# Linear attention rounds of a decoder layer: memory values as 512-column products in banks of their own, a norm by whole banks, three memory parts behind the last round, and early splits of the attention output

## The chip, the cores and the metric

The kernel runs on one core of one Trainium2 chip. Its time is the device time of one execution in microseconds (us). Before the change it is 1370.31 us, the median of 3 runs (1368.11 to 1372.6).

The core has engines that run side by side, each with its own instruction queue: PE (TensorE, matmuls; its weight loads are listed apart as PEld), DVE (VectorE), ACT (ScalarE), POOL (GpSimd) and SP (SyncE, which here only issues DMAs). PE writes to PSUM, eight banks of 128 partitions x 512 fp32 columns; DVE and ACT read them. DMA moves data between device memory and SBUF.

## The reference

```python
def reference(x, mem, norm_mix, w_in, ...):
    hn = rms_norm(h, norm_mix[l])
    gq, gk, gv, gr, ga, sq, sk, sv = jnp.split(hn @ w_in[l], split_at, axis=-1)
    o_gla = gla_mixer(gq, gk, gv, gr, ga, w_alpha[l], b_alpha[l], gla_gain[l])
    o_swa = swa_mixer(sq, sk, sv, rel_bias, sinks[l])
    h = h + jnp.concatenate([o_gla, o_swa], axis=-1) @ w_out[l]
    h = h + cross_attn(rms_norm(h, norm_cross[l]), rms_norm(mem, norm_mem[l]),
                       w_q_c[l], w_k_c[l], w_v_c[l], w_o_c[l])
    h = h + conv_ffn(rms_norm(h, norm_ffn[l]), w_up[l], conv_w[l], conv_b[l], w_down[l])
    return rms_norm(h, norm_final)

def gla_mixer(q, k, v, r, a_low, ...):       # chunks of 64 tokens, 4 heads, d_k 64, d_v 128
    ...                                      # o_intra = masked (q k) v,  o_inter = q S,  S = decay * S + k v
    o = o * lax.rsqrt(jnp.mean(o * o, axis=-1, keepdims=True) + EPS) * gla_gain
    return o.reshape(B, T, GLA_VW) * jax.nn.silu(r)
```

The layer has 1024 tokens and a width of 1024; `mem` has 256 tokens. All is fp32. Cross-attention needs `memn @ w_k` and `memn @ w_v`, 256 x 1024 each, which depend on `mem` and the weights only.

## The kernel before, in words

**Products.** Each fp32 operand is split into a high and a low part (`split`, L109 to L113: an ACT cast or scaled copy makes the high part, a DVE subtract the low part), and each product is three matmuls (`mm3`, L136 to L138: high x high, high x low, low x high). Weights come through three stage buffers `st` (`load`, L121) and are split from there into slots `w` that hold three loads. PSUM banks are handed out by role: F, S and O in the part of the program that is spoken of here (2, 4 and 2 banks).

**Stages.** First come x, its transposes and the products of its rows (`rows_a`); then the sliding-window attention in blocks of 128 queries (`swa`), whose PE order is written out by hand and in which the column products of the linear attention (`cols_gla`) fill the gaps. `swa_values` makes a block's output in one O bank, copies it to SBUF (L813) and stores it to `ow_d` with two POOL DMAs. `gate_silu` puts SiLU on the gates. Then come the gates and decays of the linear attention (`gla_gates`, `gla_decays`, L540 to L591) beside the products of the remaining value columns (`rows_b`), then `gla`.

**Rounds.** `gla` works on two blocks of 128 tokens at a time: four rounds. A round's output products (`gla_products`, L677 and L684) fill two F banks `po`. Then PE makes the states and the masked attention of the next round (L639, L662; DVE turns them into `S` at L646 and `att` at L666). `gla_norm` takes the sums of squares of the eight 128 x 128 pieces on ACT (L184), an inverse root (L170 to L178) and eight scaled copies `o` on ACT (L699). `gla_output` transposes `o` on PE (L712), multiplies by gain and gate on DVE (L715) and splits the result into `x` tiles.

**Memory parts.** `memory` is a generator. Up to its first `yield` it loads the 256 rows of `mem`, transposes and splits them (L314 and the splits L112, L113 with the gain `norm_mem`), and broadcasts the inverse roots of the rows to `mbc` (L332 on PE, a copy on ACT). After that, each `next(memory)` issues one part: eight parts for the values (four column blocks of 256, and in each the two halves of the memory tokens) and eight for the keys (four heads, two halves each). A part is 24 matmuls of 256 columns into one half of an O bank, both halves of a bank one after the other, then a split of this half and a POOL DMA to `v_d` or `k_d`. The value splits are scaled by the rows' inverse roots; a key half is first multiplied by `mbc` on DVE. In the rounds three parts stand ahead of the transposes of the round before, and one behind them; no part stands behind the last round's norm.

**Order.** On PE the order of `swa` and of the rounds is the written one (`manual_schedule`). Elsewhere, and on the other engines, a scheduler sets the order ahead of time; the chip then runs each queue in that order, and an instruction that waits holds up all that are behind it on its engine.

**After the rounds.** `swa_mix` loads the output of the sliding-window attention back in four loads of 512 KB and splits it (L109, L110); `mix_out` multiplies by `w_out` (L136 to L138 `psF<-x,w`, eight column blocks in two halves), each block's weights loaded through `st`. Cross-attention, the feed-forward network and the final norm follow.

Of the kernel before, what the change touches and what calls it, by code (L numbers as in the profile page):

```python
# [17 lines left out]
F32 = mybir.dt.float32  # L18
# [8 lines left out]
P = 128  # L27
# [33 lines left out]
class Layer:  # L61
# [237 lines left out]
    def memory(self, new):  # L299


        nc, a = self.nc, self.a
        rows = []
        for i in range(2):
            t = self.stage((P, T))
            nc.sync.dma_start(out=t, in_=a["mem"][0, i * P:(i + 1) * P, :])
            rows.append(t)
        parts = [[new("wg", [P, 3, MEM], F32R, 8) for _ in range(3)] for _ in range(2)]
# [9 lines left out]
        ssq = self.small("mssq", [P, 2], bufs=1)  # L318
        r = self.small("mrs", [P, 2], bufs=1)
        for i in range(2):  # L320
            self.sumsq(rows[i], ssq[:, i:i + 1], T)
        self.rsqrt(r, ssq, D, 2)
# [3 lines left out]
        def save(d, part, t):  # L326
# [3 lines left out]
        ps = self.bank("O")  # L330
        for i in range(2):
            nc.tensor.matmul(ps[:, i * P:(i + 1) * P], rhs=self.ident, start=True, stop=True,  # L332
                             lhsT=r[:, i:i + 1].to_broadcast([P, P]))
        bc = new("mbc", [P, MEM])
        nc.scalar.copy(out=bc, in_=ps[:, :MEM])
        yield
        wv = a["w_v_c"][0].rearrange("(kt p) c -> p kt c", p=P)
        for c in range(4):
            w = [self.load([(lambda t: t, wv[:, 4 * g:4 * g + 4, 256 * c:256 * c + 256])], (P, 4, 256), parts=2)
                 for g in range(2)]  # L340
            ps = self.bank("O")
            for i in range(2):
                tk = slice(i * P, (i + 1) * P)
                out = ps[:, i * MEM:(i + 1) * MEM]
                for k in range(NK):
                    wh, wl = w[k // 4]
                    self.mm3(out, mh[k][:, tk], ml[k][:, tk], wh[:, k % 4], wl[:, k % 4], k == 0, k == NK - 1)
                t = new("la", [P, 2, MEM], F32R, 4)
                self.split(out, t[:, 0], t[:, 1], r[:, i:i + 1])
                save(self.v_d[c], i, t)  # L350
                yield
        for h in range(4):
            ps = self.bank("O")
            for d in range(2):
                wh, wl = self.load_cols(a["w_k_c"][0], (2 * h + d) * P)
                out = ps[:, d * MEM:(d + 1) * MEM]
                for k in range(NK):
                    self.mm3(out, wh[:, k], wl[:, k], mh[k], ml[k], k == 0, k == NK - 1)
# [1068 lines left out]
```

## Time and profile before

| what | value |
|---|---|
| median of 3 runs | 1370.31 us (1368.11 to 1372.6) |
| the profiled execution | 1371.46 us, its span 1369.7 us |
| PE busy | 1324.6 us, 97% of the span |
| DVE, ACT, POOL busy | 903.2, 601.6, 73.6 us (66%, 44%, 5%) |
| gates, decays and `rows_b` | 243 to 295 us of the span |
| transposes of `mem` and first states | 295 to 301.4 us |
| the four rounds with the memory parts | 301.4 to 374.3 us |
| last norm, ahead of the last transposes | 374.3 to 384.6 us |
| `mix_out` begins | 387.59 us |

A view by windows gives, for a stretch of the span, the busy time of each engine with the number of its instructions, then the granted PE clock (1.00 is full speed), the share of the DMA engines' time and the rate in GB/s. A row of the timeline gives the start, the busy time, the engine, the line, the operation, out<-in and the shapes; in square brackets stands the idle time of the engine just before, and what released it. A row of the waits gives the total idle time, how often, and the longest. A row of groups gives, behind the count, the busy time and the mean in ns of one.

### The profile page before, as it was taken

Reading aid. Unit: us, or ns where it says so; the run is one execution under the profiler, and the core shown is the slowest. Engines: PE = TensorE matmul, PEld = TensorE weight load, DVE = VectorE, ACT = ScalarE, POOL = GpSimd, SP = SyncE. Lnnn points to the kernel's source line nnn. Section 1 sums busy time; section 2 is a strip of 40 time slices with the busy share of each in tenths; the row PEclk is TensorE's granted clock in tenths of the full one; section 3 lists DMA queues with packets and bytes.
Section 4 is the critical chain, followed back from the end, with each engine's and each line's share of the span. In section 5 each row is a group of like instructions: output and inputs, shape, how many; then the busy total and the mean of one; then the engine's idle time right before and its main releaser. Section 6 shows DMA issues by size and latency. Waiting matters only on the chain.

```text
span 1369.7 us, 17685 instructions
## 1 busy us (share of the span) xinstructions
PE 1324.6 (97%) x6735; PEld 1101.6 (80%) x6735; DVE 903.2 (66%) x1590; ACT 601.6 (44%) x1134; POOL 73.6 (5%) x126
## 2 busy tenths in 40 slices
PE   5999999999879999999999999999999999999997
PEld 5887777898868888887888888888888887888785
DVE  4626653636744543345448998888888887997776
ACT  5604443616633333345333544444444444454455
POOL 3100000001100100000110000000000000000000
PEclk9999999999989999999999999999999999999999
DMA  8441110315474421124321243322212228810204
GB/s 268 113 118 55 44 39 16 97 55 177 151 174 145 162 92 62 46 75 134 86 82 40 75 159 104 102 85 92 91 65 82 87 92 291 307 62 3 75 16 147
DMA packets 142094, 142.71 MB, mean 104 GB/s; under 512 B 15394, under 2 KB 111800, under 8 KB 142008
## 3 DMA queue, kind: packets, MB, share of 16 engines
q1 hardware_dynamic: 131446, 108.92, 26.1%
q0 software_dynamic: 9376, 30.54, 6.3%
q10 hardware_dynamic: 1186, 2.12, 0.4%
q8 instruction: 53, 0.87, 0.3%
q14 instruction: 33, 0.27, 0.1%
HBM read 106.93 MB, written 36.18 MB: 104 GB/s over the span
## 4 chain that ended last, share of the span: by engine, by line
PE 90%; DVE 4%; ACT 2%; DMA 2%; issue 1%; SPq 1%; POOL 0%; ACTq 0%; DVEq 0%; POOLq 0%
PE psS L1063 14%; PE psF L1063 13%; PE psF L136 12%; PE psF L138 12%; PE psF L137 12%; PE psF L1170 4%; PE psS L1170 4%; PE psO L136 2%; PE psT L1170 2%; PE psO L1170 2%; PE psO L137 2%; PE psO L138 1%; PE psS L136 1%; PE psS L138 1%; PE psS L137 1%; DVE w L110 1%
## 5 line engine op out<-in xcount | busy, mean ns | idle before, releaser
L109 ACT CAST w<-st 128x1024 fp32r<-128x1024 f32 (+2 forms) x171 | 144.5, 847 | 294.2 <-PE psF L137 137.4
L110 DVE TENSOR_TENSOR w<-st,w 128x1024 fp32r<-128x1024 f32 (+2 forms) x171 | 165.6, 971 | 97.4 <-ACT w L109 96.4
L136 PE MATMUL psF<-x,w 128*128 128x512 f32 x336 | 133.7, 398 | 0.4 <-DVE eb L715 0.4
L138 PE MATMUL psF<-x,w 128*128 128x512 f32 x336 | 132.2, 393 | 0.0
L137 PE MATMUL psF<-x,w 128*128 128x512 f32 x336 | 132.0, 393 | 0.0
L1092 DVE SCALAR_TENSOR_TENSOR uy<-uy,vec,uy 128x1023 f32<-128x1023 f32 (+1 forms) x88 | 112.1, 1280 | 1.0 <-ACT uy L1090 0.4
L1170 PE MATMUL psF<-w,w 128*128 128x512 f32 x330 | 92.8, 391 | 0.6 <-DVE w L110 0.6
L1170 PE MATMUL psS<-w,w 128*128 128x512 f32 x330 | 92.3, 390 | 0.0
L1063 PE MATMUL psS<-a,w 128*128 128x512 f32 x360 | 86.5, 389 | 0.0
L1063 PEld LDWEIGHTS psS<-a,w 128*128 128x128 f32 x360 | 67.6, 188 | 14.0
L1063 PE MATMUL psF<-a,w 128*128 128x512 f32 x324 | 77.8, 389 | 0.0
L136 PEld LDWEIGHTS psF<-x,w 128*128 128x128 f32 x336 | 63.7, 190 | 16.6 <-issue 3.1
L138 PEld LDWEIGHTS psF<-x,w 128*128 128x128 f32 x336 | 63.5, 189 | 14.4 <-issue 0.6
L137 PEld LDWEIGHTS psF<-x,w 128*128 128x128 f32 x336 | 63.8, 190 | 12.7
L1170 PEld LDWEIGHTS psF<-w,w 128*128 128x128 f32 x330 | 61.8, 188 | 14.3 <-DVE w L110 1.3
L1170 PEld LDWEIGHTS psS<-w,w 128*128 128x128 f32 x330 | 62.0, 188 | 12.8
L1063 PEld LDWEIGHTS psF<-a,w 128*128 128x128 f32 x324 | 60.8, 188 | 12.6
L136 PE MATMUL psF<-act,w 128*128 128x512 f32 x176 | 69.7, 396 | 0.0
L137 PE MATMUL psF<-act,w 128*128 128x512 f32 x176 | 69.1, 393 | 0.0
L138 PE MATMUL psF<-act,w 128*128 128x512 f32 x176 | 68.8, 391 | 0.0
L1090 ACT ACTIVATE uy<-uy,vec 128x1024 f32<-128x1024 f32 x44 | 54.8, 1246 | 24.7 <-DVE uy L1083 16.9
L1063 PE MATMUL psS<-act,w 128*128 128x512 f32 x240 | 57.8, 389 | 0.0
(367 smaller groups left out, 2867.1 us busy)
## 6 DMA issues: line engine op xcount, KB each, us to landing
st<-in_w_up_dram SPq DMA_DIRECT2D x44, 512.0 KB, 5.0
g_d<-uy POOLq DMA_DIRECT2D x22, 512.0 KB, 2.9
act<-in_w_down_dram SPq DMA_DIRECT2D x12, 512.0 KB, 8.5
st<-g_d SPq DMA_DIRECT2D x10, 512.0 KB, 4.5
res<-g_d SPq DMA_DIRECT2D x10, 512.0 KB, 9.5
st<-in_w_in_dram SPq DMA_DIRECT2D x9, 512.0 KB, 4.6
xt_d<-pts POOLq DMA_DIRECT2D x16, 256.0 KB, 3.1
st<-in_w_v_c_dram SPq DMA_DIRECT2D x8, 512.0 KB, 3.4
```

The source lines that it names most:

```text
L109: h = nc.scalar.copy(out=hi, in_=src)
L110: l = nc.vector.tensor_tensor(out=lo, in0=src, in1=hi.bitcast(F32), op=ALU.subtract)
L136: mm(out, lhsT=lh, rhs=rh, start=start, stop=False)
L137: mm(out, lhsT=lh, rhs=rl, start=False, stop=False)
L138: mm(out, lhsT=ll, rhs=rh, start=False, stop=stop)
L1063: nc.tensor.matmul(ps, lhsT=b[l][:, q], rhs=a[q][r], start=first and q == 0 and n == 0, stop=first and q == 3 and n == 2, skip_group_check ...
L1090: nc.scalar.activation(out=y, in_=u, func=AF.Identity, scale=self.v("cw2", j), bias=self.v("conv_b", j))
L1092: nc.vector.scalar_tensor_tensor(out=y[:, s:], in0=u[:, :T - s], scalar=self.v(nm, j), in1=y[:, s:], op0=ALU.mult, op1=ALU.add)
L1170: nc.tensor.matmul(ps[i], lhsT=g[:, l, tk], rhs=w[:, r], start=first and k == 0 and m == 0, stop=first and k == n - 1 and m == 2, skip_gro ...
```

## The change

`memory` norms the rows of `mem` first (their sums of squares, inverse roots and a multiply of the rows on ACT), so the broadcast, `mbc`, the scaling in the value splits and the multiply of the keys go. A value part is now two of the eight contraction blocks for 512 columns: 12 matmuls of 512 columns, into two whole O banks (one for each half of the memory tokens) that stay open over four parts; the four splits of these two banks come together behind the fourth. A key part has an O bank of its own. The rounds take (early, late) = (2, 0), (2, 2), (2, 2), (2, 1) parts, and the last three key parts stand behind the last round's norm and ahead of its transposes. `gla_norm` squares the two whole banks on ACT and sums on DVE, two instructions each, and its pieces are laid out by bank. The first half of the weights of `rows_b` is loaded and split ahead of the stage, into the slots `w`. `cols_gla` takes the gate columns first. `swa_values` splits its output at once (an ACT cast and a DVE subtract for the one DVE copy) and stores it with four POOL DMAs; `swa_mix` loads the split halves straight into the `x` tiles, eight loads of 512 KB with no split.

```diff
     def memory(self, new):
...
+        for i in range(2):
+            self.sumsq(rows[i], ssq[:, i:i + 1], T)
+        self.rsqrt(r, ssq, D, 2)
+        for i in range(2):
+            nc.scalar.mul(out=rows[i], in_=rows[i], mul=r[:, i:i + 1])
         parts = [[new("wg", [P, 3, MEM], F32R, 8) for _ in range(3)] for _ in range(2)]
...
+        def save(src, d, part):
+            t = new("la", [P, 2, MEM], F32R, 4)
+            self.split(src, t[:, 0], t[:, 1])
             dst = d.rearrange("p (s x m) -> p s x m", s=2, x=2)[:, :, part]
             nc.gpsimd.dma_start(out=dst, in_=t.bitcast(F32))
...
+        for c in range(0, 4, 2):
+            ps = [self.bank("O") for _ in range(2)]
+            for k in range(0, NK, 2):
+                wh, wl = self.load([(lambda t: t, wv[:, k:k + 2, 256 * c:256 * c + 512])], (P, 2, 512))
+                for q in range(2):
+                    for i in range(2):
+                        tk = slice(i * P, (i + 1) * P)
+                        self.mm3(ps[i], mh[k + q][:, tk], ml[k + q][:, tk], wh[:, q], wl[:, q], k + q == 0,
+                                 k + q == NK - 1)
+                if k == NK - 2:
+                    for i in range(2):
+                        for q in range(2):
+                            save(ps[i][:, q * MEM:(q + 1) * MEM], self.v_d[c + q], i)
                 yield
         for h in range(4):
-            ps = self.bank("O")
             for d in range(2):
+                ps = self.bank("O")[:, :MEM]
...
+                    self.mm3(ps, wh[:, k], wl[:, k], mh[k], ml[k], k == 0, k == NK - 1)
+                save(ps, self.k_d[h], d)
                 yield
...
-        self.row_chunk([(640, 384)], evac, lambda s, sh: new("wg", sh, F32R, 8))
+        n, hs, ls = self.row_weights([(640, 384)], range(4, NK), lambda s, sh: new("wg", sh, F32R, 8))
+        for i in range(NT):
+            self.row_tile(i, (n, first[1] + hs, first[2] + ls), evac)
...
-            for i in range(0, NT, 2):
-                for _ in range(3):
+            for i, (early, late) in zip(range(0, NT, 2), ((2, 0), (2, 2), (2, 2), (2, 1))):
+                for _ in range(early):
                     next(memory)
                 if i:
                     self.gla_output(i - 2, o, new)
-                next(memory)
+                for _ in range(late):
+                    next(memory)
                 po = self.gla_products(i, states)
...
                 o = self.gla_norm(po, new)
-        self.gla_output(NT - 2, o, new)
+            for _ in memory:
+                pass
+            self.gla_output(NT - 2, o, new)
...
     def gla_norm(self, po, new):
...
-        for q in range(2):
-            for h in range(4):
-                self.sumsq(po[h % 2][:, 2 * q + h // 2], ssq[:, 4 * q + h:4 * q + h + 1], P)
+        for p in range(2):
+            sq = new("lse", [P, 512], bufs=2).rearrange("p (n v) -> p n v", n=4)
+            nc.scalar.activation(out=sq, in_=po[p], func=AF.Square)
+            nc.vector.tensor_reduce(out=ssq[:, 4 * p:4 * p + 4], in_=sq, axis=mybir.AxisListType.X, op=ALU.add)
...
+        for n in range(4):
+            for p in range(2):
+                nc.scalar.mul(out=o[p][:, n], in_=po[p][:, n], mul=r[:, 4 * p + n:4 * p + n + 1])
...
     def swa_values(self, b, pts, new):
...
-        ow = new("ow", [P, 2, 2, P], bufs=2)
-        nc.vector.tensor_copy(out=ow.rearrange("p u t q -> p (u t q)"), in_=po)
...
+        ow = [new("pts", [P, 512], F32R, 9) for _ in range(2)]
+        self.split(po, *ow)
...
     def swa_mix(self):
...
-                hi, lo = self.load([(lambda t: t.rearrange("p t q -> p (t q)"), self.ow_d[u, h])], (P, 2, 512),
-                                   lambda s, sh: self.xnew("x", sh, F32R, 16))
+                hi, lo = (self.xnew("x", [P, 2, 512], F32R, 16) for _ in range(2))
+                for s, t in enumerate((hi, lo)):
+                    self.nc.sync.dma_start(out=t.bitcast(F32).rearrange("p t q -> p (t q)"), in_=self.ow_d[s, u, h])
...
                     self.gate_silu(self.swa(new, self.cols_gla(keep)))
+                    first = self.row_weights([(640, 384)], range(4))
```

The order of the instructions on the engines moves at three places. Square brackets name the engines and DMA queues whose semaphores an instruction waits for; the number behind a name tells one buffer of that name from another.

**The start of the gates, on PE.** The names are the transposes of the gate rows (`ident,ga`), the products of `rows_b` (weights `wg`, and `w` in the changed kernel) and the gates (`wal`). Before:

```order
L540 MATMUL psS_2247<-ident,ga_92 16x128 x4
L136 MATMUL psF_2410<-wg_2388,x_101 128x384 [waits Activation_49]
L136 MATMUL psF_2436<-wg_2388,x_101 128x384
L547 MATMUL psS_2253<-wal_2236,att_2239 128x256 [waits DMAHW5_49,DMAHW4_49,DVE_49]
```

After:

```order
L529 MATMUL psS_2291<-ident,ga_92 16x128 x4
L136 MATMUL psF_2442<-w_2262,x_101 128x384
L137 MATMUL psF_2442<-w_2263,x_101 128x384
...
L137 MATMUL psF_2468<-w_2269,x_107 128x384
L138 MATMUL psF_2468<-w_2268,x_108 128x384
L136 MATMUL psF_2442<-wg_2432,x_109 128x384 [waits Activation_49]
L136 MATMUL psF_2468<-wg_2432,x_109 128x384
L536 MATMUL psS_2297<-wal_2280,att_2283 128x256 [waits DMAHW7_49,DMAHW6_49,DVE_49]
```

Between the transposes of the gate rows and the first gate product stood two matmuls of `rows_b`; now 26 stand there, 24 of them from the weights that were split ahead.

**The hand-over of the value banks in the second round, on ACT.** `o` are the scaled copies of the norm, `la` the high parts of the value splits, `x` that of `gla_output`, `psO_2772` and `psO_2773` the two banks that the first four value parts filled. Before, in a round whose bank took two parts, one such split stood between the inverse root and the norm's copies:

```order
L172 ACTIVATE rs_y_2977<-rs_t_2976 128x8 [waits Activation_49]
L112 ACTIVATE la_3036<-psO_3011,mrs_2677 128x256 [waits DMASW2_49,PE_49]
L699 ACTIVATE o_2985<-psF_2889,grs_2974 128x128 [waits DVE_49]
```

After:

```order
L693 ACTIVATE o_2897<-psF_2811,grs_2885 128x128
L109 CAST la_2942<-psO_2772 128x256 [waits DMASW3_49,DMASW2_49,PE_49]
L109 CAST w_3114<-st_3112 128x1024 [waits DMAHW7_49,PE_49]
L109 CAST la_2946<-psO_2772 128x256 [waits DVE_49]
L109 CAST la_2950<-psO_2773 128x256 [waits DMASW7_49,DMASW6_49,PE_49]
L109 CAST x_2650<-eb_2963 128x2x256 [waits DVE_49]
L109 CAST la_2954<-psO_2773 128x256 [waits DVE_49]
```

All four splits of the two banks stand behind the norm's eight copies. PE's next value part opens both banks again and waits for them:

```order
L705 MATMUL psS_2968<-ident,o_2897 128x128 [waits Activation_49]
L136 MATMUL psO_2978<-w_2982,wg_2684 128x512 [waits DVE_49,PE_49]
...
L136 MATMUL psO_2979<-w_2982,wg_2684 128x512 [waits DVE_49,PE_49]
```

**The end of the last round, on PE.** Before:

```order
L684 MATMUL psF_3705<-S_3483,gq_1574 64x128
L712 MATMUL psS_3770<-ident,o_3759 128x128 [waits PE_49,Activation_49]
...
L136 MATMUL psF_3847<-x_3792,w_3843 128x512 [waits DVE_49,PE_49]
```

After:

```order
L676 MATMUL psF_3475<-S_3304,gq_2154 64x128
L136 MATMUL psO_3529<-wg_2684,w_3532 128x256 [waits DVE_49]
...
L136 MATMUL psO_3564<-wg_2684,w_3567 128x256 [waits DVE_49]
...
L136 MATMUL psO_3599<-wg_2684,w_3602 128x256 [waits DVE_49]
...
L705 MATMUL psS_3634<-ident,o_3519 128x128 [waits PE_49,Activation_49]
```

Where the transposes stood next behind the last round's products, three key parts now stand between.

On SP, the loads of the attention output now come behind the first weights of `mix_out`, eight in a row:

```order
L121 DMA st_3696<-in_w_out_dram 64x4x128 x2
L819 DMA x_3655<-ow_d 128x1024 [waits DMASW6_49,DMASW2_49]
...
L819 DMA x_3668<-ow_d 128x1024 [waits DMAHW3_49,DMASW5_49,DMASW1_49]
L121 DMA st_3768<-in_w_out_dram 128x4x128 [waits DMAHW4_49,DVE_49,Activation_49]
```

Before, four loads of `ow_d` into `st` stood ahead of the first weights of `mix_out`.

More of the change, by code (lines that the diff above doesn't have):

```diff
@@ L327, in save @@
             dst = d.rearrange("p (s x m) -> p s x m", s=2, x=2)[:, :, part]
             nc.gpsimd.dma_start(out=dst, in_=t.bitcast(F32))
-        ps = self.bank("O")
[L331 to L335, printed above, removed]
         yield
         wv = a["w_v_c"][0].rearrange("(kt p) c -> p kt c", p=P)
[L338 to L350, printed above, removed]
@@ L418, in row_weights @@
         hs, ls = [], []
-        for g in range(0, NK, step):
-            m = min(step, NK - g)
+        for g in range(ks.start, ks.stop, step):
+            m = min(step, ks.stop - g)
             pieces, at = [], 0
@@ L437, in row_tile @@
         evac(i, ps)
-    def row_chunk(self, cols, evac, alloc=None):
-        weights = self.row_weights(cols, alloc)
-        for i in range(NT):
-            self.row_tile(i, weights, evac)
     def rows_a(self, keep, new):
@@ L696, in gla_norm @@
         o = [new("o", [P, 4, P], bufs=2) for _ in range(2)]
-        for q in range(2):
-            for h in range(4):
-                self.nc.scalar.mul(out=o[q][:, h], in_=po[h % 2][:, 2 * q + h // 2],
-                                   mul=r[:, 4 * q + h:4 * q + h + 1])
+        for n in range(4):
+            for p in range(2):
+                nc.scalar.mul(out=o[p][:, n], in_=po[p][:, n], mul=r[:, 4 * p + n:4 * p + n + 1])
         return o
@@ L811, in swa_values @@
                                  rhs=pts[2 * j + g], start=j == 0, stop=j == nb - 1)
-        ow = new("ow", [P, 2, 2, P], bufs=2)
-        nc.vector.tensor_copy(out=ow.rearrange("p u t q -> p (u t q)"), in_=po)
-        for u in range(2):
-            dst = self.ow_d[u, b // 4].rearrange("p (t q) -> p t q", t=2)[:, :, (b % 4) * P:(b % 4 + 1) * P]
-            nc.gpsimd.dma_start(out=dst, in_=ow[:, u])
+        ow = [new("pts", [P, 512], F32R, 9) for _ in range(2)]
+        self.split(po, *ow)
+        for s, t in enumerate(ow):
+            for u in range(2):
+                dst = self.ow_d[s, u, b // 4].rearrange("p (t q) -> p t q", t=2)[:, :, (b % 4) * P:(b % 4 + 1) * P]
+                src = t[:, 256 * u:256 * u + 256].bitcast(F32).rearrange("p (t q) -> p t q", t=2)
+                nc.gpsimd.dma_start(out=dst, in_=src)
     def swa_mix(self):
@@ L1350, in run @@
                     self.gla_decays(new)
-                    self.rows_b(new)
+                    self.rows_b(new, first)
                     self.gla(new)
```

33 lines of the change are left out of this document (11 added, 22 removed).

## The prediction

> **What bounds the kernel now.** I read the page first: which engine is full, and where in the span it is not. Then the waits of PE between 296 and 396 us, then the windows around the waits, because a wait also costs what the clock does after it.
>
> ```profile
> PE 1324.6 (97%) x6735; PEld 1101.6 (80%) x6735; DVE 903.2 (66%) x1590; ACT 601.6 (44%) x1134; POOL 73.6 (5%) x126
> PE   5999999999879999999999999999999999999997
> PEclk9999999999989999999999999999999999999999
> PE 90%; DVE 4%; ACT 2%; DMA 2%; issue 1%; SPq 1%; POOL 0%; ACTq 0%; DVEq 0%; POOLq 0%
> ```
>
> PE is busy for 97% of the span and the chain that ended last runs through it for 90%. So PE sets the end, and only three things count: matmul time taken away, PE idle time, and time at a low clock. Freed time on DVE or ACT counts where PE waits for them. Each slice is 34.2 us. The two below 9 in the middle of the PE row, the eleventh and twelfth, are 342 to 411 us; the 8 in the clock row is the twelfth.
>
> ```profile
> PE psS L712 <- ACT o L699: 10.3, 1, 10.3
> PE psO L136 <- DVE la L113: 3.6, 4, 1.2
> PE psO L136 <- ACT w L109: 2.0, 2, 1.0
> PE psF L136 <- DVE eb L715: 0.4, 1, 0.4
> ```
>
> One wait stands out: 10.3 us before the last transposes of the linear attention, for the norm's copies on ACT. The second halves of the value banks cost four waits of up to 1.2 us, the weights' splits two.
>
> ```profile
> 249.00:255.50 6.50, 6.50 (x18) 5.17 (x17) 4.21 (x6) 5.51 (x11) 0.00 (x0) 0.50 0.87 290
> 301.40:374.30 72.90, 67.36 (x745) 64.56 (x744) 51.06 (x115) 43.26 (x122) 10.15 (x15) 1.00 0.49 158
> 374.30:384.60 10.30, 0.00 (x1) 0.00 (x1) 4.95 (x10) 6.61 (x23) 0.68 (x1) 0.70 1.02 236
> 384.60:391.40 6.80, 6.30 (x17) 4.56 (x18) 4.93 (x8) 3.92 (x10) 0.00 (x0) 0.50 0.74 146
> ```
>
> In the 72.90 us of the rounds PE is busy for 67.36: 5.5 us idle at full clock. The next 10.30 us are empty, and for 6.30 busy us behind them the clock is 0.50: half of that, 3.15 us, is lost as well. The gates show the same clock for 6.50 us.
>
> **A, the gates.**
>
> ```profile
> 244.48 1.04 PE L540 MATMUL psS<-ident,ga 128*16 128x128 f32 x8 [0.82 <-DVE ow L813]
> 245.81 0.62 PE L136 MATMUL psF<-wg,x 128*128 128x384 f32 x2 [0.28 <-ACT wg L109]
> L799 ACT COPY pts<-psS 128x512 f32<-128x512 f32 x30 | 15.4, 597 | 10.6 <-PE psS L797 10.6
> L813 DVE COPY ow<-psO 128x512 f32<-128x512 f32 x8 | 5.5, 687 | 3.6 <-PE psO L810 3.6
> ```
>
> The transposes of the gate rows take the bank of the last attention output. Before, one DVE copy frees it. Now an ACT cast does (nearest row 0.597 us) and then a DVE subtract (nearest row the copy, 0.687 us): the wait grows from 0.82 by 0.6. The 0.28 for the split of the weights goes, since 24 matmuls on weights split in good time stand next. These fill the place in which the clock fell. If it stays at 1.00, 3.25 us come back (half of 6.50); if it falls as before, nothing. I take half, 1.6, since the first wait gets longer. Sum: 1.6 + 0.3 - 0.6 = 1.3 saved, between -0.3 and 2.9.
>
> The clock is 0.50 here although the longest idle time just before is 0.82 us. [...]
>
> **B, the broadcast.**
>
> ```profile
> 300.76 0.68 PE L332 MATMUL psO<-ident,mrs 128*128 128x128 f32 x4 [0.32 <-DVE wg L113]
> 295.75 1.94 ACT L112 ACTIVATE wg<-psO,vec 128x256 fp32r<-128x256 f32 x4 [20.21 <-PE psO L314]
> ```
>
> It goes with its wait: 1.0 saved. The norm of the `mem` rows moves ahead of their transposes, two more ACT multiplies of 128x1024; ACT is idle for 20 us ahead of the transposes' splits, and hides them. If it did not, they would cost 2.1 (two of the 1.05 us casts below).
>
> **C, the rounds.** Matmul time first, by start times of neighbours: 21 matmuls of 256 columns, 11 steps of 512.
>
> ```profile
> 308.80 0.28 PE L136 MATMUL psO<-w,wg 128*128 128x256 f32 x1
> 311.13 0.28 PE L138 MATMUL psO<-w,wg 128*128 128x256 f32 x1
> 399.73 0.39 PE L138 MATMUL psF<-x,w 128*128 128x512 f32 x1
> 402.23 0.39 PE L137 MATMUL psF<-x,w 128*128 128x512 f32 x1
> ```
>
> The first two rows are 20 steps apart: 0.1165 us each. The other two give 0.227. The value parts go from 192 x 0.1165 = 22.4 to 96 x 0.227 = 21.8: 0.6 saved. A part is 2.8 us before, 2.7 now; a key part stays 2.8. The old waits (5.5 us), and the restart that each shows (0.39 against 0.28, six times, 0.7 us), end with the half banks: 6.2 saved.
>
> Against that stands the norm. Before, three parts (8.4 us) lie between a round's attention and the transposes; now two do.
>
> ```profile
> 318.47 0.28 ACT L184 ACTIVATE junk<-psF 128x128 bf16<-128x128 f32 x1 [1.47 <-PE psF L684]
> 320.30 0.38 PE L136 MATMUL psO<-w,wg 128*128 128x256 f32 x1
> 319.33 2.16 DVE L646 SCALAR_TENSOR_TENSOR S<-S,dec,psS 128x128 f32<-128x128 f32 x8 [1.49 <-PE psS L639]
> 321.40 1.36 DVE L666 COPY_PREDICATED att<-mask_att,psS 128x512 f32<-128x512 int32 x2
> 322.65 0.16 DVE L170 TENSOR_SCALAR rs_v<-gssq 128x8 f32<-128x8 f32 x1
> 324.13 2.17 ACT L699 ACTIVATE o<-psF,grs 128x128 f32<-128x128 f32 x8 [0.25 <-DVE grs L178]
> L877 ACT ACTIVATE sq<-res 128x512 f32<-128x512 f32 x14 | 8.6, 618 | 0.0
> L910 DVE TENSOR_REDUCE cmx<-psS 128x2 f32<-128x512 f32 x16 | 10.7, 687 | 2.1 <-PE psS L138 2.1
> ```
>
> Count from the first square (318.47 in that round). Two whole-bank squares at 0.618 are done at 1.24, two reductions at 0.687 behind them at 2.0. In the changed DVE order `S` and `att` come next, 3.32 (319.33 to 322.65), and then the inverse root: 5.3. From `rs_v` to the first copy is 1.48: 6.8. The eight copies take 2.17; the first transposes need six of them: 8.4. PE, meanwhile, starts its two parts at 1.83 and is through at 7.2. So each of three rounds waits 1.2: 3.6 lost.
>
> Next, the banks. All four value splits of both banks stand behind the copies in ACT's queue, with a weight split between them.
>
> ```profile
> 383.24 1.05 ACT L109 CAST w<-st 128x1024 fp32r<-128x1024 f32 x1 [1.31 <-DMA st<-in_w_out_dram]
> L112 ACT ACTIVATE la<-psO,mrs 128x256 fp32r<-128x256 f32 x8 | 3.8, 471 | 5.7 <-PE psO L138 5.6
> L113 DVE SCALAR_TENSOR_TENSOR la<-psO,mrs,la 128x256 fp32r<-128x256 f32 x8 | 3.8, 480 | 2.7 <-ACT la L112 2.7
> ```
>
> Copies done at 9.0; then 0.47 + 1.05 + 0.47 on ACT and 0.48 on DVE: the first bank is free at 11.5. PE would start the fifth value part behind the last four transposes (eight are 2.57 at half clock in D's row, so four 0.6) at 9.6: 1.9 lost. The second bank needs another 0.47, the `x` cast (0.6, as L799) and 0.47: free at 13.0, wanted 0.7 after the first: 0.9 lost. The first key part, behind the eighth value part, needs one bank: 1.9 lost. Together 4.7; at best half, if the scheduler's order is met by idle engines, at worst as much again. Waiting behind these matmuls on PE are the remaining parts, and nobody but the norm waits for them. C in all: 0.6 + 6.2 - 3.6 - 4.7 = -1.5, between 2.6 and -5.6 (half or one and a half of the waits).
>
> **D, the last norm.**
>
> ```profile
> 384.60 2.57 PE L712 MATMUL psS<-ident,o 128*128 128x128 f32 x8 [10.31 <-ACT o L699]
> ```
>
> Three key parts, 8.4 us, now stand where PE was idle. The chain of the last round has no `S` or `att` on DVE: 2.0 + 1.48, a weight split of 1.05 that stands between on ACT, 2.17: copies done at 6.7, within 8.4. But the third part reuses the bank of the first, whose split stands behind the copies: free at 6.7 + 0.47 + 0.48 = 7.6, wanted behind two parts, at 5.6: 2.0 lost. The 0.4 for `eb` stays. Saved: 10.3 + 3.15 - 2.0 = 11.4. Without the cover the old wait less the work that moved would be left.
>
> **E, the clock in the rounds.** The waits of C sit together, 1.2, 1.9 and 0.9 within 5 us at one place. Like the gates' they could cost a stretch of half clock, 3 us; the old waits of the same size (up to 1.2) cost none. Taken: 0.7, between 0 and 3.
>
> **F, early splits.** Eight ACT casts (0.6 each) and 16 more POOL DMAs lie in a stage, 60 to 243 us, whose slices are all 9 in the PE row, so PE's work hides them; only the last block is waited for (in A). The eight loads of 512 KB are costed with the rivals. The start-up and all behind the rounds keep their order. Zero, and at worst the price of the third rival.
>
> **Sum.** 1.3 + 1.0 - 1.5 + 11.4 - 0.7 = 11.5. Against the profiled execution, 1371.46 us (1.15 above the median of the runs), that is 1360.0; put on the median, 1370.3 - 11.5 = 1358.8, say 1359.
>
> **The rivals.**
>
> *The waits don't come.* ACT and DVE are 59% and 70% busy in the rounds, and a queue that runs ahead would halve the waits of C (4.1) and of D (1.0), and the clock stays up (A 1.6 more, E 0.7): 7.4 more, 1351. For it: before, the largest wait for a split was 1.2. Against: the splits stand behind the copies in a fixed queue.
>
> *The stall only moves.* The waits of C and D double (10.3 more): 1369, hardly a gain. For it: cover was taken from three rounds to fill one. Against: each step is costed from rows, and a doubling needs steps that I don't see.
>
> *The loads of the attention output become the bound, the slower side.*
>
> ```profile
> st<-ow_d SPq DMA_DIRECT2D x4, 512.0 KB, 3.9
> st<-in_w_out_dram SPq DMA_DIRECT2D x16, 128.0 KB, 4.8
> ```
>
> SP issues the first weights of `mix_out`, then eight loads, once the split of the third-last key weights has freed a stage buffer; that split waits for the slot of the sixth-last key part. From there to `mix_out` lie five key parts (14.0), the last products and two rounds' transposes, some 18; the last four loads are needed 24 x 0.227 = 5.4 us into it. Nine loads in 23.4 us are 2.6 each. At 4.8 each, one behind the other, they end 19.8 late: 1379. It is slower than before from 3.9 each. For it: 3.9 is the time to landing of such a load. Against: that is a time with others in flight; the window from 374.30 moved 236 GB/s, 2.2 us for 512 KB.
>
> *The clock swings.* If the waits between banks let the clock alternate between 0.5 and 1 through the 73 us, a mean of 0.75 costs 67.4/0.75 - 67.4 = 22 us: 1381. Against: six such waits before, at 1.00. [...]
>
> **How the numbers follow.** Forecast 0.66; waits absent 0.16; stall moved 0.10; loads 0.04; clock 0.04. A measurement of this kernel tells about 0.3% (4.1 us) from nothing: faster means below 1366.2, slower above 1374.4. The forecast and the first rival lie below; of the second I give 0.02 to faster and 0.08 to no change; the last two are slower, with 0.01 of each near no change. Faster 0.84, same 0.10, slower 0.06. The range takes in the bounds of A (+1.6, -1.6), half of the bounds of C (+2.1, -2.1), D and E: 1351 to 1366.
>
> **What would show it.** Right: the wait before the last transposes gone and the clock at 1.00 behind it; in each of three rounds a wait of about 1.2 us for `o`, and waits of 2 to 3 us for `la` where a pair of value banks is opened again; the rounds, from the first part to the first matmul of `mix_out`, at about 78 us instead of 86. Wrong: waits for `x` from `ow_d` on PE, a clock row below 9 between 300 and 380 us, or a wait for `o` above 3 us in a round.

## The result, and the profile after

| | before | after |
|---|---|---|
| median | 1370.62 us (1368.11 to 1372.6) | 1361.11 us (1360.55 to 1362.74) |
| profiled execution, its span | 1371.46, 1369.7 us | 1360.55, 1358.8 us |
| ratio of the times | | 0.9933, 95% interval 0.9917 to 0.9949 |

The kernel is 9.5 us faster: more than the 0.3% (4.1 us) that the prediction counts as no change, inside the range of 1351 to 1366, and 2 us above the predicted 1359. The page of the changed kernel: busy time of the engines, PE's share by slices, its clock by slices.

```profile
PE 1320.4 (97%) x6635; PEld 1093.1 (80%) x6635; DVE 899.9 (66%) x1578; ACT 593.7 (44%) x1075; POOL 84.7 (6%) x142
PE   5999999999999999999999999999999999999997
PEclk8999999999999999999999999999999999999998
```

The hole in the eleventh and twelfth slice is closed. Its waits of PE between 240 and 400 us (total, times, longest):

```profile
PE psO L136 <- DVE la L110: 5.2, 5, 1.7
PE psS L529 <- DVE pts L110: 1.4, 1, 1.4
PE psO L136 <- DVE wg L113: 1.3, 1, 1.3
PE psF L136 <- PE psS L705: 0.9, 1, 0.9
PE psS L705 <- ACT o L693: 0.8, 3, 0.3
PE psO L320 <- DVE wg L113: 0.8, 1, 0.8
```

The one wait of 10.3 us for `o` is three of 0.3 at most; the largest sum is now for `la`, the splits of the value and key banks. The windows of the same profile (us; busy time of PE, PEld, DVE, ACT, POOL; clock; DMA share; GB/s):

```profile
251.00:257.00 6.00, 6.00 (x29) 4.83 (x28) 2.15 (x3) 4.61 (x8) 0.00 (x0) 1.00 0.38 141
299.58:366.90 67.32, 62.32 (x577) 53.86 (x578) 48.31 (x105) 30.96 (x69) 8.88 (x13) 0.95 0.52 161
366.90:378.50 11.60, 9.79 (x80) 9.34 (x80) 5.39 (x14) 5.55 (x17) 1.83 (x3) 1.00 1.06 372
378.50:385.00 6.50, 6.46 (x29) 5.40 (x30) 3.66 (x6) 2.26 (x3) 0.23 (x1) 1.00 1.10 345
```

The gates and the start of `mix_out` run at 1.00, where 0.50 stood before. But the rounds are at 0.95, where 1.00 stood. By stages of the span, from the rows of the timeline that open them:

| stage | before | after | difference |
|---|---|---|---|
| up to the transposes of the gate rows | 244.48 | 245.68 | +1.20 |
| gates, to the first transposes of `mem` | 50.63 | 47.23 | -3.40 |
| to the first value part | 6.30 | 6.67 | +0.37 |
| rounds and last norm, to `mix_out` | 86.18 | 78.96 | -7.22 |
| the rest | 982.11 | 980.26 | -1.85 |
| sum | 1369.7 | 1358.8 | -10.9 |

Of the +1.20, 0.62 is the longer wait of the gate rows (1.44 for 0.82); the rest lies within the spread of the start, since that row begins between 243.9 and 245.9 us in the profiles below that have the same wait of 1.44. The -1.85 has the size of the half clock that no longer lies on the first 3.8 us of `mix_out` (1.9); but in the ten profiles that start `mix_out` at full clock this stage takes between 979.6 and 982.3 us, so it is not resolved.

Where the rounds gave time back is in these rows of PE's timeline. A hand-over is the place where PE opens a PSUM bank again and waits until the splits have emptied it. The rows at 321.87 and 322.30 are neighbours in the fifth value part:

```profile
316.35 1.10 PE L705 MATMUL psS<-ident,o 128*128 128x128 f32 x7 [0.27 <-ACT o L693]
319.16 0.47 PE L136 MATMUL psO<-w,wg 128*128 128x512 f32 x1 [1.70 <-DVE la L110]
320.55 0.47 PE L136 MATMUL psO<-w,wg 128*128 128x512 f32 x1 [0.45 <-DVE la L110]
...
321.87 0.63 PE L137 MATMUL psO<-w,wg 128*128 128x512 f32 x1
322.30 0.63 PE L138 MATMUL psO<-w,wg 128*128 128x512 f32 x1
...
340.99 0.36 PE L136 MATMUL psO<-wg,w 128*128 128x256 f32 x1 [1.70 <-DVE la L110]
373.67 0.39 PE L136 MATMUL psO<-wg,w 128*128 128x256 f32 x1 [0.97 <-DVE la L110]
378.54 0.47 PE L136 MATMUL psF<-x,w 128*128 128x512 f32 x1 [0.88 <-PE psS L705]
```

The two hand-overs behind the value banks cost 2.15 (1.70 and 0.45) and 1.70 us, a third one 0.39 (at 360.90). The two neighbours are 0.43 us apart, where 512 columns take 0.23 in the first two value parts: about 2 us behind the first hand-over the clock is halved (0.51 from 321.10 to 324.40). Windows of the same profile at both hand-overs:

```profile
319.20:325.00 5.80, 5.35 (x16) 3.94 (x17) 3.79 (x8) 2.18 (x4) 2.06 (x3) 0.71 0.80 258
341.00:347.00 6.00, 6.00 (x38) 6.00 (x39) 4.13 (x8) 2.49 (x5) 2.06 (x3) 0.72 0.80 255
```

0.29 of 5.8 us and 0.28 of 6.0 is 1.7 us each: 3.4 us go to the clock, beside the 3.85 of waiting at these two. The norm of the first round, on ACT and DVE, and that of the last on ACT:

```profile
308.29 1.09 ACT L686 ACTIVATE lse<-psF 128x512 f32<-128x512 f32 x2 [2.03 <-PE psF L676]
308.92 1.28 DVE L687 TENSOR_REDUCE gssq<-lse 128x4 f32<-128x512 f32 x2 [1.40 <-ACT lse L686]
310.11 2.15 DVE L638 SCALAR_TENSOR_TENSOR S<-S,dec,psS 128x128 f32<-128x128 f32 x8
312.18 1.35 DVE L658 COPY_PREDICATED att<-mask_att,psS 128x512 f32<-128x512 int32 x2
314.90 2.17 ACT L693 ACTIVATE o<-psF,grs 128x128 f32<-128x128 f32 x8
...
366.89 1.08 ACT L686 ACTIVATE lse<-psF 128x512 f32<-128x512 f32 x2 [1.65 <-PE psF L676]
...
370.73 2.17 ACT L693 ACTIVATE o<-psF,grs 128x128 f32<-128x128 f32 x8
```

In the first round the copies begin 6.61 us behind the first square: the reductions stand ahead of `S` and `att`, and the inverse root behind these. In the last round, without `S` and `att`, it is 3.84.

### The profile page after: what moved, and what is told of

Same layout as the page of the kernel before. It is cut to its first block, busy times and chain, and to the rows that moved or that the text cites. A ratio compares the mean times of both kernels' runs of the same rounds, so it can differ in the third digit from the quotient of the medians.

```text
span 1358.8 us, 17462 instructions
## 1 busy us (share of the span) xinstructions
PE 1320.4 (97%) x6635; PEld 1093.1 (80%) x6635; DVE 899.9 (66%) x1578; ACT 593.7 (44%) x1075; POOL 84.7 (6%) x142
## 4 chain that ended last, share of the span: by engine, by line
PE 90%; DVE 3%; DMA 3%; ACT 2%; issue 1%; POOL 0%; SPq 0%; ACTq 0%; DVEq 0%; POOLq 0%
PE psS L1059 13%; PE psF L1059 13%; PE psF L136 12%; PE psF L138 12%; PE psF L137 12%; PE psF L1166 5%; PE psS L1166 5%; PE psT L1166 2%; PE psO L1166 2%; PE psO L136 1%; PE psS L136 1%; PE psS L138 1%; PE psS L137 1%; PE psO L137 1%; PE psO L138 1%; DMA act<-in_w_down_dram 1%
## 5 line engine op out<-in xcount | busy, mean ns | idle before, releaser
L138 PE MATMUL psF<-act,w 128*128 128x512 f32 x176 | 68.7, 390 | 0.0
```

Source lines behind the costliest of these rows:

```text
L138: mm(out, lhsT=ll, rhs=rh, start=False, stop=stop)
```

## The experiments

### The old order of the parts in the changed kernel

```diff
-            for i, (early, late) in zip(range(0, NT, 2), ((2, 0), (2, 2), (2, 2), (2, 1))):
+            for i, (early, late) in zip(range(0, NT, 2), ((3, 1), (3, 1), (3, 1), (3, 1))):
```

> The changed kernel with the rounds' old order: three parts ahead of the transposes and one behind them in each round, nothing behind the last norm. Theory 1 (the two bank hand-overs that stand right behind a norm cost about 7 us in the changed kernel: 1.70 + 0.45 + 1.70 us of waiting and two stretches of 3.3 us at half clock; the three parts at the end save the last stall): here the first value pair ends with the first round, so both hand-overs are covered, and a last stall of about 6 us with 3 us of clock behind it comes back: 1361.1 - 7 + 9 = about 1363 us. Rival (the order at the end is the whole gain, the hand-overs cost little): 1369 to 1371 us, about the kernel before.

Measured: 1362.46 us (1361.61 to 1365.69), 0.9941 of the kernel before (0.9926 to 0.9956). The end of the last round on PE:

```profile
375.16 0.47 PE L705 MATMUL psS<-ident,o 128*128 128x128 f32 x1 [3.93 <-ACT o L693]
378.12 0.77 PE L136 MATMUL psF<-x,w 128*128 128x512 f32 x1 [0.16 <-PE psS L705]
```

The stall is back, at 3.9 us and 0.56 behind it, and `mix_out` starts at half clock (0.77 for 0.47), yet the time is only 1.4 us longer, which the intervals don't resolve. Both pairs of value banks are now handed over under a round's products and cost no wait. But the hand-overs in the rounds are not all covered, as theory 1 had it: two key parts wait in their place, and the clock falls behind each (the window behind the second, from 360.10, reads 0.72 too):

```profile
339.30 0.39 PE L136 MATMUL psO<-wg,w 128*128 128x256 f32 x1 [2.30 <-DVE la L110]
360.10 0.40 PE L136 MATMUL psO<-wg,w 128*128 128x256 f32 x1 [1.81 <-DVE la L110]
339.30:345.30 6.00, 6.00 (x38) 6.00 (x39) 2.40 (x5) 2.02 (x3) 1.38 (x2) 0.72 0.83 246
```

So the total of theory 1 came, and its stall was smaller and its rounds dearer than it said. In the changed kernel the new order gives at the end little more than it takes in the rounds: without it the kernel is still 8.8 us faster than before. The last stall is 4.5 us instead of 10.3 because the copies begin 3.44 us behind the first square (371.30 to 374.74), where the kernel before needed 9.84 (374.35 to 384.19), with casts of the attention output and of weights between, three of which waited for their loads (0.43, 1.66 and 1.31 us). No run separates here what the new norm and what the early splits did.

### The new order alone

```diff
 # the kernel before
-                for _ in range(3):
+                for _ in range(early):
                     next(memory)
...
-                next(memory)
+                for _ in range(late):
+                    next(memory)
...
+            for _ in memory:
+                pass
+            self.gla_output(NT - 2, o, new)
```

> The kernel before with nothing changed but the order of the parts: (2, 0), (2, 2), (2, 2), (2, 1) and three key parts behind the last norm. Theory 1 (the tail is where the time came from, and products of 512 columns, banks and norm gave and took about the same): the stall of 10.3 us goes but for 2 to 3 us, and so does the half clock behind it: about 1360 us, as the changed kernel. Rival (the new banks and the new norm are needed for it): the key halves that share a bank wait again behind the norm's copies, 1365 us or more.

Measured: 1368.68 us (1367.17 to 1369.8), 0.9982 (0.9973 to 0.9992). Two rows of PE:

```profile
346.49 0.36 PE L136 MATMUL psO<-wg,w 128*128 128x256 f32 x1 [1.95 <-DVE lse L360]
379.67 0.55 PE L136 MATMUL psO<-wg,w 128*128 128x256 f32 x1 [4.29 <-DVE lse L360]
```

The rival holds: the stall moved from the transposes to the second half of a key bank, whose release (the multiply by `mbc`) comes late. The clock falls behind both (0.72 from 346.49 to 352.49, 0.66 from 379.70 to 387.65). The order alone is worth 2.6 us.

### The new order with a bank for each key half

```diff
 # the kernel before, with the new order
-            ps = self.bank("O")
             for d in range(2):
+                out = self.bank("O")[:, :MEM]
                 wh, wl = self.load_cols(a["w_k_c"][0], (2 * h + d) * P)
-                out = ps[:, d * MEM:(d + 1) * MEM]
```

> The kernel before with the new order of the parts (1368.7 us alone) and one bank for each key half, still multiplied by mbc on DVE. Theory 1 (the new order alone failed because the second half of a key bank waits for the split of the first, which stands behind the norm's copies: 1.95 and 4.29 us): these waits go or fall to 1 to 2 us, 1362 to 1365 us. Rival (the casts of the attention output, which stand among the squares of the last round, hold up the norm): 1367 to 1369 us.

Measured: 1362.53 us (1361.15 to 1363.65), 0.9942 (0.9927 to 0.9957). What is left on PE at the end:

```profile
377.03 0.33 PE L714 MATMUL psS<-ident,o 128*128 128x128 f32 x1 [3.90 <-ACT o L701]
```

Both waits on the key banks are gone, and 8.1 us are saved: the two edits together are enough for most of the 9.5. They are not the only way to it, since the first experiment kept the old order and saved 8.8; the savings don't add up. The banks without the order were not run. The 3.9 us that remain are for the norm, among whose squares the casts of the attention output now stand in ACT's order, one of them waiting 2.29 us for its load (at 372.87); so the rival's mechanism is there as well, at 3.9 us.

### Four parts first

```diff
-            for i, (early, late) in zip(range(0, NT, 2), ((2, 0), (2, 2), (2, 2), (2, 1))):
+            for i, (early, late) in zip(range(0, NT, 2), ((4, 0), (2, 2), (2, 0), (2, 1))):
```

> The changed kernel with (4, 0), (2, 2), (2, 0), (2, 1) parts in the rounds and three behind the last: the two pairs of value banks are now full at the end of a round's parts, ahead of its products, instead of behind a norm. Theory 1: waits for la of 1.70, 0.45 and 1.70 us and both stretches of half clock go, the norm starts no later: 7 us less, about 1354 us. Rival (the splits, which now stand ahead of the norm's squares on ACT, only move the wait to the norm and the transposes): 1359 to 1362 us.

Measured: 1356.26 us (1356.01 to 1359.27), 0.9897 (0.9882 to 0.9911), 4.9 us less than the changed kernel. Its waits:

```profile
PE psS L705 <- ACT o L693: 1.8, 4, 0.7
PE psO L136 <- DVE la L110: 1.4, 2, 1.0
```

The hand-overs are gone from the list (the 1.4 are two waits of key parts), and 1.0 us more is spent on `o`. From the transposes of `mem` to `mix_out` the profile has 79.28 us, the changed kernel's 85.63. That is 6.35 of the expected 7; the gates took 1.6 us more in this execution (below), and the rest 2.0 more. The clock stays at 1.00 from 298 to 396 us.

### Work in the place of the wait

```diff
                     self.gla_output(i - 2, o, new)
+                    if i < 6:
+                        junk = self.bank("F")
+                        for _ in range(13):
+                            nc.tensor.transpose(junk[:, :P], self.ident, self.ident)
```

This adds transposes whose result nobody reads; nothing of the computation is left out.

> The changed kernel with 13 more transposes of the identity (into a spare F bank, read by nobody) behind the transposes of the first three rounds, so that PE has work in the place of the 1.7 us wait ahead of the fifth value part and of the first key part. Theory 1 (the half clock for 3.3 us behind these places comes from PE's idle time there): the waits turn into work of the same length, the clock stays at 1.00 and some 3 us are saved, less what the filler adds at the third place (about 1 us): 1358 to 1359 us. Rival (the clock falls for another reason): the same dips, 1361 to 1363 us.

Measured: 1358.65 us (1355.58 to 1360.36), 0.9907 (0.9889 to 0.9924). The first hand-over and the windows of 8 us behind both:

```profile
322.50 0.47 PE L136 MATMUL psO<-w,wg 128*128 128x512 f32 x1 [0.29 <-DVE la L110]
322.50:330.50 8.00, 7.54 (x39) 6.13 (x40) 5.54 (x9) 3.27 (x5) 2.06 (x3) 1.00 0.75 232
342.79:350.79 8.00, 8.00 (x76) 7.88 (x80) 6.38 (x10) 3.83 (x7) 2.74 (x4) 1.00 0.74 230
```

The fifth value part starts as late behind the transposes as before, but the clock stays at 1.00 and the stage from `mem` to `mix_out` is 3.1 us shorter (82.54 for 85.63). So PE's own idle time at the hand-overs took the clock down (windows of 8 us from there read 0.79 twice in the changed kernel, behind waits of 1.70, and 1.00 twice here, behind 0.29 and 0.28), and useless work there is a gain in the rounds. The weight lies on the first hand-over: at the second the clock stayed up without a filler in two other profiles (last section). The whole time is 2.5 us less by the medians, with intervals that overlap.

### The norm by pieces

```diff
         for p in range(2):
-            sq = new("lse", [P, 512], bufs=2).rearrange("p (n v) -> p n v", n=4)
-            nc.scalar.activation(out=sq, in_=po[p], func=AF.Square)
-            nc.vector.tensor_reduce(out=ssq[:, 4 * p:4 * p + 4], in_=sq, axis=mybir.AxisListType.X, op=ALU.add)
+            for n in range(4):
+                self.sumsq(po[p][:, n], ssq[:, 4 * p + n:4 * p + n + 1], P)
```

> The changed kernel with the old sums of squares: eight pieces on ACT (L184) instead of two whole-bank squares and two DVE reductions. Theory 1 (in the rounds the reductions stand ahead of S and att on DVE and delay the norm's copies by about 0.8 us; behind the last round, where DVE has nothing else, whole banks are 1.2 us quicker): the two hand-over waits of 1.70 shrink to about 0.9 each, the waits for o go, the wait of the last key part grows from 0.97 to about 2.2: 1357 to 1361 us, the lower end if the half clock behind the hand-overs goes as well. Rival (the norm by whole banks is a gain in every round): slower by 2 to 3 us, 1363 to 1364.

Measured: 1356.7 us (1355.43 to 1359.96), 0.9897 (0.988 to 0.9914): 4.4 us less than the changed kernel. The first square and the copies of that round, the first hand-over, and the window behind it:

```profile
309.32 0.28 ACT L184 ACTIVATE junk<-psF 128x128 bf16<-128x128 f32 x1 [2.04 <-PE psF L676]
315.00 2.17 ACT L692 ACTIVATE o<-psF,grs 128x128 f32<-128x128 f32 x8
319.25 0.47 PE L136 MATMUL psO<-w,wg 128*128 128x512 f32 x1 [1.36 <-DVE la L110]
319.25:327.25 8.00, 7.54 (x39) 6.13 (x40) 5.55 (x9) 3.27 (x5) 2.06 (x3) 1.00 0.75 225
```

The copies begin 5.68 us behind the first square instead of 6.61, though the squares themselves take longer. The hand-over waits fall only from 1.70 to 1.36, not to 0.9; but that was enough for the clock to stay at 1.00 in this profile, which by the rows is the larger part of the gain (3.4 us, beside 2.8 of waiting). For the rounds theory 1 holds: fewer instructions made the norm slower, since two of them went onto the engine that the round was waiting for. For the last round it doesn't. The norm is slower there with pieces, as expected (6.29 us from the first square to the copies, for 3.84), yet the last key part's wait of 0.97 did not grow to 2.2 but is gone: the bank's split now stands ahead of the copies on ACT, in the time of the inverse root.

### Both together

Four parts first, the sums of squares by pieces in the first three rounds, and whole banks in the last round only.

```diff
+            if whole:
                 sq = new("lse", [P, 512], bufs=2).rearrange("p (n v) -> p n v", n=4)
...
+            else:
+                for n in range(4):
+                    self.sumsq(po[p][:, n], ssq[:, 4 * p + n:4 * p + n + 1], P)
...
-                o = self.gla_norm(po, new)
+                o = self.gla_norm(po, new, i + 2 == NT)
```

> The kernel with four parts in the first round, (4, 0), (2, 2), (2, 0), (2, 1) and three behind, and the sums of squares by pieces in the first three rounds, by whole banks in the last only. Theory 1 (reductions ahead of S and att delay the norm): the waits for o, 1.8 us in all with whole banks in every round (1356.3 us), go: 1354 to 1355 us. Rival (no difference or slower): 1356 to 1358 us.

Measured: 1352.29 us (1351.21 to 1352.88), 0.9863 (0.9846 to 0.9879). It was measured again beside the next kernel:

> The best version again (four parts first, three behind the last round, sums of squares by pieces except in the last round), beside the next kernel on one chip: 1352 us, 0.986 of the kernel before.

Measured: 1353.96 us (1352.16 to 1356.32), 0.9884 (0.9864 to 0.9903). All its waits of PE from 240 to 400 us in the first of the two:

```profile
PE psS L529 <- DVE pts L110: 1.4, 1, 1.4
PE psO L136 <- DVE wg L113: 1.4, 1, 1.4
PE psO L136 <- DVE la L110: 1.4, 2, 1.0
PE psF L136 <- PE psS L709: 0.9, 1, 0.9
PE psO L320 <- DVE wg L113: 0.8, 1, 0.8
```

No wait for `o` is left. This version beats both kernels: 17 to 20 us below the kernel before on the same chips, 7 to 9 below the changed kernel's median. The 1.0 in the third row is the wait of the last key part, which the norm by pieces in every round did not have; four parts first with pieces in the last round too was not run.

### The early weights of `rows_b`

```diff
-        n, hs, ls = self.row_weights([(640, 384)], range(4, NK), lambda s, sh: new("wg", sh, F32R, 8))
+        weights = self.row_weights([(640, 384)], range(NK), lambda s, sh: new("wg", sh, F32R, 8))
...
-                    first = self.row_weights([(640, 384)], range(4))
```

In the changed kernel:

> The changed kernel with the first half of the weights of rows_b loaded and split inside the stage again, as before. Theory 1 (the 24 matmuls on early weights hold up the clock in the gates, in most executions): the stage from the transposes of the gate rows to those of mem, 47.2 us in the changed kernel's profile and 47.2, 48.8 and 51.5 in three profiles with the same code there, is 50.5 us again with a clock of 0.50 for some 6 us: 1363 to 1364 us. Rival (the clock there goes by chance, or by the longer first wait): 1361 us, and a stage of 47 to 49 us.

Measured: 1361.37 us (1360.55 to 1363.6), 0.993 (0.9915 to 0.9945). In the best version:

> The best version with the first half of the weights of rows_b inside the stage again. Theory 1 (what the early weights save in the gates, 2 us on the mean of the profiles with a clock that falls in some executions only, they lose again where the value weights then come among the splits of mem, 1.35 against 0.31 us of waiting and 1.0 us of stage): within 2 us of the version before it, 1351 to 1354 us. Rival (the clock in the gates is worth its full 3 us): 1355 us or more.

Measured: 1354.38 us (1353.19 to 1354.77), 0.9881 (0.9867 to 0.9896), for 1353.96 with them on the same chip. Without the early weights, in the changed kernel, the window of the gates, and the first transposes of `mem` and the first value part:

```profile
250.00:253.00 3.00, 2.37 (x7) 1.40 (x6) 1.09 (x3) 2.94 (x6) 0.00 (x0) 0.50 0.93 337
296.12 1.03 PE L320 MATMUL psO<-ident,st 128*128 128x128 f32 x8
301.76 0.47 PE L136 MATMUL psO<-w,wg 128*128 128x512 f32 x1 [0.31 <-DVE wg L113]
```

The low clock is back in the gates, which take 50.99 us, as expected; but from there to the first value part it is 5.64 us where the early weights give 6.67. In the whole time nothing is seen of it in either pair. The rival of the first run was right about the total, at 1361, and wrong about the stage.

The gates are not the same in every execution. In the profiles with the early weights and the same code there they take 47.23, 47.23, 48.79, 48.82, 48.83, 48.83 and 51.54 us, a mean of 48.8; the window of the longest, the kernel with the filler, has a wait that the others lack:

```profile
256.22 2.04 PE L554 MATMUL psS<-la,mask_rev 128*128 128x256 f32 x4 [1.59 <-DVE la L543]
```

The five longer ones have a stretch of half clock that the two of 47.23 lack. It begins between 253.9 and 255.6 us, and windows of 3 us put it at 3.4 us in four of them and 6.8 in the longest; without the early weights it is 6.8 in all five profiles. One of the four, the norm by pieces:

```profile
252.00:263.00 11.00, 11.00 (x51) 9.57 (x50) 5.84 (x10) 9.41 (x19) 0.00 (x0) 0.84 0.08 30
```

So with the early weights the stretch is half as long in four of the seven profiles, gone in two, and as long as without them in one. What decides between them is open; the profile of the changed kernel happened to be one of the two best.

### The late splits

The copy, the two DMAs a block, the four loads and the splits of the attention output as before, in the changed kernel.

```diff
-        ow = [new("pts", [P, 512], F32R, 9) for _ in range(2)]
-        self.split(po, *ow)
+        ow = new("ow", [P, 2, 2, P], bufs=2)
+        nc.vector.tensor_copy(out=ow.rearrange("p u t q -> p (u t q)"), in_=po)
...
```

> The changed kernel with the attention output copied whole, stored with two DMAs a block, loaded back with four loads and split in the last round, as before. Theory 1 (the early splits are worth nothing on the path: the first wait of the gates is 0.6 longer with them; the casts in the last round are covered by the three key parts, and one key split comes ahead of the norm's copies): 1360 to 1362 us, the wait of the gate rows 0.82 instead of 1.44. Rival (the casts, each 1.05 us and each behind a load, hold up the norm's copies and PE waits for o again): 1364 us or more.

Measured: 1361.43 us (1358.58 to 1363.5), 0.9927 (0.9909 to 0.9945). The gate rows wait 0.82 again, and the end of the rounds a little longer:

```profile
246.04 1.04 PE L529 MATMUL psS<-ident,ga 128*16 128x128 f32 x8 [0.82 <-DVE ow L806]
381.10 0.47 PE L136 MATMUL psF<-x,w 128*128 128x512 f32 x1 [1.58 <-DVE eb L708]
```

0.62 less there, 0.70 more here (1.58 for 0.88), and 0.53 more at the last key part (1.50 for 0.97): the early splits are worth nothing that can be measured in the changed kernel.

## Why the prediction was right, and where its steps were not

**The bound.** Right. What PE waited for and at which clock is what moved the time. From the first value part to `mix_out`, the 86.18 us before hold 16.25 of waits and 1.3 of half clock, the 78.96 after 6.84 and 3.4: without them, 68.6 and 68.7 are left.

**A, the gates: half of the clock, 1.3.** The profile gave the upper end: 3.40 less the 0.62 of the wait that lies ahead of it, 2.8. The mean of the seven profiles gives 50.63 - 48.8 = 1.8, less 0.62: 1.2. So the half was right on the mean, and in four of the seven profiles half of the stretch is what is left. In the five profiles without the early weights the clock stands at 0.50 from 250 to 253 us, and PE's longest wait between 240 us and there is 0.82 us in three of them and 1.44 in two.

**B, the broadcast: 1.0 saved.** Wrong: 0.37 lost. The step that failed is that the path loses the broadcast and gets nothing in its place. The broadcast and its wait did go; but with the slots taken by the early weights, the third value weights come late, and their cast and split stand among the splits of `mem` on ACT and DVE: 1.35 of waiting for `wg`. Without the early weights it is 0.31, and the stage is 0.66 shorter than before.

**C, the rounds: 1.5 lost.** By the rows it was 0.5 saved: 5.5 of old waits, less 0.75 for `o`, less 4.24 at the hand-overs. The 1.3 for wider products and restarts didn't show. The 0.6 rested on 0.227 a step, taken from `mix_out`; the 22 steps from 299.89 to 305.01 in the first two value parts take 0.233 each, so 96 of them are 22.3 against 22.4. The wait for `o` was put at 1.2 a round and was 0.27, 0.28 and 0.20. The chain itself was well sized (copies 6.61 behind the first square, 6.8 predicted). What failed is "the first transposes need six of them": each transpose follows its own copy, PE arrives when the copies are half done (at 316.08, where they run from 314.90 to 317.07), and loses only what it outruns them by. The hand-overs were put at 2.8 and 1.9 and measured 2.15 and 1.70, with the 0.39 that wasn't foreseen; the mechanism was right, down to its place.

**D, the last norm: 11.4 saved.** The last key part waited 0.97 where 2.0 was said, because the chain was 0.7 us shorter (copies done at 372.90, 6.0 behind the first square; most of the weight split beside them fits into the wait for the inverse root) and PE came 0.2 later; `mix_out` waited 0.88 instead of 0.4. 10.3 + 3.15 - 0.97 - 0.46 = 12.0.

**E, the clock in the rounds: 0.7, between 0 and 3.** Right in kind, too small, and outside its own bounds: 3.4 us at two places. The step that failed is the reading of the row at 1.00 in the rounds before: waits of 1.2 us, each alone between parts of 2.8, had cost no clock; a wait of 1.70 in a row with one of 0.27 and transposes did. The filler (0.29 us of waiting there, the clock at 1.00) and the four parts first (no wait there, 1.00) show that it is this idle time.

**F, early splits and loads: nothing.** Right. The eight loads were issued from 361.2 to 365.8 us and took 11.3 us to land at most, so all lay there by 377.1, ahead of `mix_out` at 378.54, and PE waited for no `x` from `ow_d`. So the third rival did not come; the clock's swing through all rounds did not come either, though the clock did fall behind waits between banks, at two places (0.71 and 0.72 in the windows there).

**The rivals.** Of the first, that the waits don't come, the part on `o` held and the part on the banks did not. The second, that the stall only moves, is what the new order does without banks for the key halves. That the new order needs a bank for each key half was not in the prediction as a condition.

**The sum.** Of C, D and E 9.2 was predicted; the last two stages of the table give 7.22 + 1.85 = 9.1. The errors cancelled: 2.0 more in C and 0.6 more in D against 2.7 more for the clock. That the total came within 2 us is partly luck.

## What to carry to other kernels

A stall at the end of a loop is filled by holding back independent work, but the work must not need a resource (here a PSUM bank) whose release stands behind the stalled chain in another engine's queue: in the kernel before, the order alone gave 2.6 us, with a bank for each piece 8.1. Let a pair of banks fill up at a point that is followed by other long work, not right behind a norm: moving two parts gained 4.9 us. Count instructions on the engine that the chain waits for: two whole-bank reductions on DVE made the norm slower than eight small sums on ACT wherever DVE had the recurrence to do (6.61 us to the copies for 5.68), and quicker where it had nothing (3.84 for 6.29); but a quicker norm did not mean a shorter wait there, since the order on ACT changed with it.

## What the runs showed of the hardware

The clock halved behind idle times of PE that are shorter than the stretch it then stayed down: in the changed kernel 1.70 us of idle time, and 3.4 us of half clock. In the rounds, up to the first matmuls of `mix_out`, it fell at each of the seven waits of 1.81 us and more, at four of six waits of 1.70, and at none of 1.61 and less. (1.70 is in the changed kernel and in those without early weights and with late splits. The fall came during the wait or within 2 us behind it, where in the changed kernel a wait of 0.45 follows.) 1.36 and 0.46 did not bring it down in the kernel with the norm by pieces. In the gates of the kernel before it fell behind waits of 0.82 and 0.28, some 2.8 us after the second (1.00 from 244 to 247 us, 0.77 to 250, 0.50 to 253). At the second hand-over the same 1.70 brought it down in one profile of three:

```profile
342.50:350.50 8.00, 8.00 (x76) 7.88 (x80) 6.37 (x10) 3.82 (x7) 2.74 (x4) 1.00 0.78 233
```

(This row is of the changed kernel without early weights; the changed kernel has 0.72 there.) So the price of a wait of 1.70 us was the wait, or the wait and some 1.7 us more, and a single profile cannot tell which will be the rule.

The stretches of half clock measured here are 3.4 us long, or twice or four times that. With the clock at 0.50, the lost share times the window times two is the length: 0.28 x 6.0 x 2 = 3.4 us in the rows above. Taken so over windows of 2 us, the stretches that end before the kernel's last matmuls are 6.8, 6.8 and 13.7 us long in the kernel before, the 13.7 around its last norm, and 6.8, 3.4 and 3.4 in the changed kernel. In the gates, windows of 3 us give 3.4 four times and 6.8 seven times, in the eleven profiles that have a stretch there. What sets this length, and why the same wait brought the clock down in one execution and not in another, no run here shows.
